# Loading and storing the sample caches of layer B from SyncE's queue, in 112 and 15 rows

## The chip, the core and the metric

The kernel runs on one core of a Trainium2 chip. The metric is the device time of one execution in microseconds (us). The engines are TensorE (PE in the profile, with PEld for its weight loads), VectorE (DVE), ScalarE (ACT), GpSimd (POOL) and SyncE (SP, which here issues DMAs and nothing else). "q" behind an engine's name means its queue of instructions, with the waits and the DMA issues.

## The reference

One inference step of a two-layer decoder trunk with width 1024, for a prompt of 1024 tokens and for 8 sample sequences with one new token each; both groups share the weights. All 1032 tokens go through the same matrix products.

```
layer A: x += hgrn2_mixer(rmsnorm(x)) @ w_a_out;  x += sq_relu_mlp(rmsnorm(x))
k, v = split(rmsnorm(x) @ w_kv)                      # 4 heads of 64
layer B: q = rmsnorm(x) @ w_b_q                      # 16 heads of 64
  prompt: attention over a sliding window of 128, T5 bias, a sink per head
  sample: kk = concat(cache_k_win, k_new); vv = concat(cache_v_win, v_new)
          the same attention over the last 128 rows
          cache_k_win_sample, cache_v_win_sample = kk[:, 1:], vv[:, 1:]
  x += attention @ w_b_out;  x += sq_relu_mlp(rmsnorm(x))
y = rmsnorm(x)
```

The sample caches have the shape (8, 128, 4, 64) in float32. The new window of a sequence is rows 1 to 127 of its old cache and one new row. It is read by the sample's attention and is also an output.

## The kernel before, in words

Tiles are 128 rows by 1032 tokens, with the model width on the partitions. A matrix product in float32 is made of three products of split operands (`job`, L386: high by high, low by high, high by low). The weights go from DRAM into two raw buffers (`load_raw`, L165, issued by SP), are split by ACT and DVE (L181 and L182 with a norm's gain, L186 and L189 without) into a pool of five units, and are read by PE.

The stage around the change is layer B's attention, about 1300 to 1640 us of the span. Its dense work is a list of steps: the products for K, V and the eight query groups, then `first_pass` (the first half of the w_b_out product). `mix` lays a list of side steps between them. The side steps come from `ticks(m, extra)`, one tick for each query group m of two heads, with eight blocks of 128 queries each: `scores(B)` (PE at L1193, then DVE and ACT), `turn(B - 3)` (PE transposes the probabilities, L1226; ACT and DVE split them, L1229 and L1230) and `weighted(B - 4)` (PE at L1244). For every two blocks `scores` ends with a reciprocal on DVE (L1212) and two multiplications of the probabilities by it on POOL (L1216). POOL also adds halves of the attention's output (L1254), loads the bias tiles (L1180), and writes the prompt's caches (L1128) and the new rows of the samples to a DRAM tile `newrows` (L1129).

`extras` (L1369) puts the sample's work into the ticks. In tick 4, `window` (L1265) is called four times, for K and V and for each half of the batch (four sequences). It takes a tile `win` with the 128 window rows on the partitions and four sequences of 256 columns side by side, loads 127 rows from the cache (L1270) and the last row from `newrows` (L1271). In tick 5 come `keys_t` (transposes of the windows of K, L1289), the scores and the products with the windows of V (`av`, L1319) for the first half of the heads, and `window_out` for K, which stores the whole tile to the output (L1274). In tick 6 come the stores of V, in tick 7 the second half of the heads. All these DMAs are issued by POOL.

In layer A and in the MLPs the order on PE, DVE and ACT is that of the source. In this stage it is not: `order.close()` (L1095) hands it to the framework's planner until L1388. The planner places the instructions of each queue by modelled times when the kernel is built, and each queue then runs in that order and waits where an operand is not there.

Of the kernel before, what the change touches and what calls it, by code (L numbers as in the profile page):

```python
# [9 lines left out]
F32 = mybir.dt.float32  # L10
# [7 lines left out]
P = 128  # L18
# [24 lines left out]
def trunk(ctx: ExitStack, tc: tile.TileContext, x_prompt, x_sample, state_hgrn, cache_k, cache_v,  # L43
# [4 lines left out]
    V, S, G, PE, SY = nc.vector, nc.scalar, nc.gpsimd, nc.tensor, nc.sync  # L48
# [8 lines left out]
    def uid(name):  # L57
        n_tile[0] += 1
        return f"{name}_{n_tile[0]}"

    def A(dt=F32, name="a"):
        return ap.tile([P, T], dt, tag="a", name=uid(name))
# [1043 lines left out]
    newrows = dp.tile([2, NS, 2 * P], F32, name="newrows")  # L1106
# [152 lines left out]
    win, smp = {}, {}  # L1259
    caches = {"k": (cache_k, 0, kc_sample), "v": (cache_v, 1, vc_sample)}  # L1260

    def tb(t):
        return t[:, :1024].rearrange("p (b c) -> p b c", c=256)

    def window(which, i):  # L1265
        cache, n, _ = caches[which]
        t = A(F32, "win")
        win[which, i] = t
        bs = slice(4 * i, 4 * i + 4)
        G.dma_start(out=tb(t)[0:P - 1], in_=cache[bs, 1:P].rearrange("b t h d -> t b (h d)"))  # L1270
        G.dma_start(out=tb(t)[P - 1:P], in_=newrows[n:n + 1, bs, :])  # L1271

    def window_out(which, i):
        G.dma_start(out=caches[which][2][4 * i:4 * i + 4].rearrange("b t h d -> t b (h d)"), in_=tb(win[which, i]))  # L1274

    def sample_steps(jt):

# [88 lines left out]
    def split_head(m):  # L1366
        heads_a[m] = split(aTs[m])

    extras = {4: [lambda w=w, i=i: window(w, i) for w in "kv" for i in range(2)],  # L1369
              5: s0[:2] + s1[:2] + s0[2:] + [lambda i=i: window_out("k", i) for i in range(2)],  # L1370
              6: [lambda i=i: window_out("v", i) for i in range(2)] + [lambda m=m: split_head(m) for m in range(NK // 2)],
              7: s1[2:5]}
    side = ticks(NK - 1, extras[NK - 1])
# [147 lines left out]
```

## Time and profile before

| | |
|---|---|
| Median of 3 runs | 2416.85 us (2414.13 to 2417.04) |
| Profiled execution, its own time | 2414.3 us |
| Its span, first to last instruction | 2412.6 us |
| PE busy | 2322.5 us, 96% of the span |
| DVE busy | 1619.8 us, 67% |
| ACT busy | 935.2 us, 39% |
| POOL busy | 231.2 us, 10% |

The busy time of an engine is the time in which one of its instructions runs. Issuing a DMA is not counted as busy on the page, but it appears in the timelines with the time that it held its engine. The granted clock is the share of TensorE's full clock of 2.4 GHz that the throttle allowed. A share of the whole span says little on a stage of 100 us; for that, the views are cut into windows.

### The profile page before, as it was taken

Reading aid. Unit: us, or ns where it says so; the run is one execution under the profiler, and the core shown is the slowest. Engines: PE = TensorE matmul, PEld = TensorE weight load, DVE = VectorE, ACT = ScalarE, POOL = GpSimd, SP = SyncE. Lnnn points to the kernel's source line nnn. Section 1 sums busy time; section 2 is a strip of 40 time slices with the busy share of each in tenths; the row PEclk is TensorE's granted clock in tenths of the full one; section 3 lists DMA queues with packets and bytes.
Section 4 is the critical chain, followed back from the end, with each engine's and each line's share of the span. In section 5 each row is a group of like instructions: output and inputs, shape, how many; then the busy total and the mean of one; then the engine's idle time right before and its main releaser. Section 6 shows DMA issues by size and latency. Waiting matters only on the chain. (4 is left out here: it accounts for less than half of the span.)

```text
span 2412.6 us, 40091 instructions
## 1 busy us (share of the span) xinstructions
PE 2322.5 (96%) x16389; PEld 2288.8 (95%) x16389; DVE 1619.8 (67%) x3154; ACT 935.2 (39%) x1914; POOL 231.2 (10%) x221
## 2 busy tenths in 40 slices
PE   8999999999999999999999995799999999999998
PEld 7899999999999999999999985699999999999998
DVE  5666676675476676766757884686467677676765
ACT  6444454543323322322325684564323223322322
POOL 0111111120000000000000245340000000000002
PEclk9999999999999999999999998899999999999999
DMA  3222222234111121111121112201111111121122
GB/s 124 72 63 63 63 63 64 72 70 73 44 45 53 44 57 49 45 53 45 53 62 45 42 37 48 65 27 40 40 45 53 53 54 44 45 62 45 44 62 80
DMA packets 206392, 133.23 MB, mean 55 GB/s; under 512 B 18122, under 2 KB 198532, under 8 KB 206208
## 3 DMA queue, kind: packets, MB, share of 16 engines
q1 hardware_dynamic: 186464, 107.04, 15.1%
q0 software_dynamic: 19392, 23.04, 4.2%
q8 instruction: 129, 2.11, 0.4%
q10 hardware_dynamic: 352, 0.59, 0.1%
q14 instruction: 55, 0.45, 0.1%
HBM read 115.97 MB, written 14.50 MB: 54 GB/s over the span
## 5 line engine op out<-in xcount | busy, mean ns | idle before, releaser
L386 PE MATMUL ps<-h,w 128*128 128x344 f32 (+1 forms) x6144 | 1161.8, 323 | 8.4 <-DVE y L882 3.1
L386 PEld LDWEIGHTS ps<-h,w 128*128 128x128 f32 x6144 | 996.3, 189 | 15.2 <-issue 8.7
L386 PE MATMUL ps<-l,w 128*128 128x344 f32 x3072 | 659.3, 322 | 2.6 <-DVE tmp L424 2.6
L386 PEld LDWEIGHTS ps<-l,w 128*128 128x128 f32 x3072 | 511.9, 189 | 4.3 <-DVE tmp L424 3.2
L1013 DVE TENSOR_TENSOR y<-ps,y 128x516 f32<-128x516 f32 x392 | 271.2, 692 | 125.6 <-PE ps L1008 123.1
L1008 PE MATMUL ps<-l,w 128*128 128x258 f32 x1120 | 226.0, 283 | 0.0
L1008 PE MATMUL ps<-b,w 128*128 128x258 f32 x1568 | 225.1, 283 | 0.0
L1022 DVE SCALAR_TENSOR_TENSOR r<-ps,R 128x688 f32<-128x688 f32 x126 | 81.7, 690 | 209.1 <-PE ps L386 209.1
L1008 PE MATMUL ps<-t,w 128*128 128x258 f32 x1344 | 218.5, 285 | 0.0
L219 ACT ACTIVATE w<-wr 128x512 fp32r<-128x512 f32 x168 | 99.6, 623 | 292.3 <-DVE wr L231 218.5
L1028 ACT ACTIVATE r<-r 128x1032 f32<-128x1032 f32 x63 | 67.3, 1068 | 367.6 <-DVE r L1022 367.6
L1008 PEld LDWEIGHTS ps<-b,w 128*128 128x128 f32 x1568 | 205.5, 190 | 0.0
L1008 PEld LDWEIGHTS ps<-t,w 128*128 128x128 f32 x1344 | 185.0, 190 | 0.3
L1008 PEld LDWEIGHTS ps<-l,w 128*128 128x128 f32 x1120 | 173.9, 190 | 0.0
L186 ACT ACTIVATE w<-wr 128x512 fp32r<-128x512 f32 x168 | 102.5, 622 | 132.3 <-PE ps L1008 74.6
L189 DVE TENSOR_TENSOR w<-wr,w 128x512 fp32r<-128x512 f32 x168 | 115.9, 708 | 54.5 <-ACT w L186 54.4
L182 DVE SCALAR_TENSOR_TENSOR w<-wr,cols,w 128x128 fp32r<-128x128 f32 x352 | 127.0, 403 | 30.7 <-ACT w L181 30.1
L227 DVE TENSOR_TENSOR w<-wr,w 128x512 fp32r<-128x512 f32 x168 | 115.3, 686 | 42.4 <-ACT w L219 42.3
L231 DVE TENSOR_TENSOR wr<-wr 128x256 f32<-128x256 f32 x280 | 118.0, 422 | 6.2
L181 ACT ACTIVATE w<-wr,cols 128x128 fp32r<-128x128 f32 x352 | 115.3, 393 | 12.7 <-PE ps L386 10.2
L963 ACT ACTIVATE t<-r 128x1032 fp32r<-128x1032 f32 x56 | 59.6, 1065 | 91.4 <-DVE r L985 91.4
L1461 POOL TENSOR_TENSOR sqc<-sqc,sq 128x384 f32<-128x384 f32 (+1 forms) x18 | 16.7, 927 | 749.1 <-ACT sq L1460 745.8
(295 smaller groups left out, 2731.7 us busy)
## 6 DMA issues: line engine op xcount, KB each, us to landing
wr<-in_w_up_dram SPq DMA_DIRECT2D x64, 512.0 KB, 4.2
wr<-in_w_down_dram SPq DMA_DIRECT2D x112, 256.0 KB, 3.1
wr<-in_w_a_in_dram SPq DMA_DIRECT2D x32, 512.0 KB, 4.2
si<-in_state_hgrn_dram POOLq DMA_DIRECT2D x8, 512.0 KB, 4.7
xin<-in_x_prompt_dram SPq DMA_DIRECT2D x8, 512.0 KB, 6.1
vb<-vrows POOLq DMA_DIRECT2D x8, 512.0 KB, 4.0
out_dram<-si POOLq DMA_DIRECT2D x8, 512.0 KB, 4.2
wr<-in_w_a_out_dram SPq DMA_DIRECT2D x8, 512.0 KB, 3.6
```

The source lines that it names most:

```text
L181: S.activation(out=hi[:, j], in_=part[:, j], func=AF.Copy, scale=g[:, k:k + 1])
L182: V.scalar_tensor_tensor(out=lo[:, j], in0=part[:, j], scalar=g[:, k:k + 1], in1=f32(hi[:, j]), op0=ALU.mult, op1=ALU.subtract)
L186: S.activation(out=hi, in_=part, func=AF.Copy)
L189: V.tensor_tensor(out=lo, in0=part, in1=f32(hi), op=ALU.subtract)
L219: S.activation(out=hi, in_=src, func=AF.Copy)
L227: V.tensor_tensor(out=lo, in0=src, in1=f32(hi), op=ALU.subtract)
L231: return lambda: V.tensor_tensor(out=out, in0=in0, in1=in1, op=op)
L386: PE.matmul(st["o"][c], lhsT=ww[:, col:col + P], rhs=xx[:, cs], start=((k, i) == first and also is None), stop=((k, i) == last))
L1008: PE.matmul(o[:, c, :CQ], lhsT=ww, rhs=xx[:, c * CQ:(c + 1) * CQ], start=(begins and k == 0 and i == 0), stop=(k == 1 and i == 2), skip_gr ...
L1013: V.tensor_tensor(out=y, in0=o[:, :, :CQ], in1=y, op=ALU.add)
L1022: V.scalar_tensor_tensor(out=v(r), in0=p, scalar=0.0, in1=v(R), op0=ALU.max, op1=ALU.mult)
L1028: S.activation(out=rs[-1], in_=rs[-1], func=AF.Square)
```

## The change

Three edits. `window` issues its load from SP instead of POOL, and as two DMAs, of 112 rows and of 15 rows, instead of one of 127. The copy of the new row moves from `window` into a function of its own, `window_new`, also on SP; in tick 4 the four calls of `window` come first and then the four of `window_new`, where before each copy followed its load. `window_out` issues its store from SP. The bytes and the tiles are the same.

```diff
--- before.py
+++ after.py
@@ -1263,15 +1263,18 @@
         return t[:, :1024].rearrange("p (b c) -> p b c", c=256)
 
     def window(which, i):
-        cache, n, _ = caches[which]
-        t = A(F32, "win")
+        cache, t = caches[which][0], A(F32, "win")
         win[which, i] = t
         bs = slice(4 * i, 4 * i + 4)
-        G.dma_start(out=tb(t)[0:P - 1], in_=cache[bs, 1:P].rearrange("b t h d -> t b (h d)"))
-        G.dma_start(out=tb(t)[P - 1:P], in_=newrows[n:n + 1, bs, :])
+        for r in (slice(0, 112), slice(112, P - 1)):
+            SY.dma_start(out=tb(t)[r], in_=cache[bs, r.start + 1:r.stop + 1].rearrange("b t h d -> t b (h d)"))
+
+    def window_new(which, i):
+        n = caches[which][1]
+        SY.dma_start(out=tb(win[which, i])[P - 1:P], in_=newrows[n:n + 1, 4 * i:4 * i + 4, :])
 
     def window_out(which, i):
-        G.dma_start(out=caches[which][2][4 * i:4 * i + 4].rearrange("b t h d -> t b (h d)"), in_=tb(win[which, i]))
+        SY.dma_start(out=caches[which][2][4 * i:4 * i + 4].rearrange("b t h d -> t b (h d)"), in_=tb(win[which, i]))
 
     def sample_steps(jt):
 
@@ -1366,7 +1369,7 @@
     def split_head(m):
         heads_a[m] = split(aTs[m])
 
-    extras = {4: [lambda w=w, i=i: window(w, i) for w in "kv" for i in range(2)],
+    extras = {4: [lambda w=w, i=i, f=f: f(w, i) for f in (window, window_new) for w in "kv" for i in range(2)],
               5: s0[:2] + s1[:2] + s0[2:] + [lambda i=i: window_out("k", i) for i in range(2)],
               6: [lambda i=i: window_out("v", i) for i in range(2)] + [lambda m=m: split_head(m) for m in range(NK // 2)],
               7: s1[2:5]}
```

## Rows read from the trace of the kernel before

**Rows 1.** The page's slices: PE's busy tenths and its granted clock, 60.3 us a slice.

```profile
PE   8999999999999999999999995799999999999998
...
PEclk9999999999999999999999998899999999999999
```

**Rows 2.** Stretches of 1470 to 1541 us; columns are in the first row.

```profile
core 0: us, PE busy (x) PEld busy (x) DVE busy (x) ACT busy (x) POOL busy (x), PEclk, DMA share, GB/s
...
1470.10:1494.60 24.50, 0.00 (x1) 0.00 (x0) 1.75 (x9) 2.17 (x9) 6.54 (x5) 0.60 0.20 41
1494.60:1507.20 12.60, 12.56 (x78) 12.28 (x78) 5.79 (x22) 8.32 (x25) 10.03 (x8) 0.83 0.35 70
1507.20:1522.60 15.40, 0.03 (x1) 0.00 (x0) 2.84 (x9) 0.70 (x2) 2.62 (x4) 0.57 0.25 70
1522.60:1541.40 18.80, 18.75 (x128) 18.09 (x129) 13.97 (x44) 12.83 (x38) 9.19 (x11) 0.90 0.32 111
```

**Rows 3.** Waits from 1440 to 1560 us: total, times, longest.

```profile
PE ps L1226 <- POOL pr L1216: 40.0, 2, 24.5
...
POOL win L1270 <- issue: 17.9, 1, 17.9
...
POOL out_dram L1274 <- issue: 15.1, 1, 15.1
```

**Rows 4.** POOL's timeline: start, duration, instruction, idle time before it.

```profile
1460.41 4.62 POOL L1270 DMA_DIRECT2D win<-in_cache_k_win_dram  x1
...
1466.31 4.62 POOL L1270 DMA_DIRECT2D win<-in_cache_k_win_dram  x1
...
1489.33 4.58 POOL L1270 DMA_DIRECT2D win<-in_cache_v_win_dram  x1 [17.89 <-issue]
1493.98 1.60 POOL L1216 TENSOR_TENSOR pr<-pr,es 128x256 f32<-128x256 f32 x2
...
1496.94 2.04 POOL L1216 TENSOR_TENSOR pr<-pr,es 128x512 f32<-128x512 f32 x2
1498.92 4.64 POOL L1270 DMA_DIRECT2D win<-in_cache_v_win_dram  x1
...
1519.92 1.58 POOL L1274 DMA_DIRECT2D out_dram<-win  x2 [15.08 <-issue]
1521.56 2.03 POOL L1216 TENSOR_TENSOR pr<-pr,es 128x512 f32<-128x512 f32 x2
```

**Rows 5.** DVE's timeline: the reciprocals of the softmax denominators.

```profile
1468.51 0.16 DVE L1212 RECIPROCAL es<-es 128x4 f32<-128x4 f32 x1
...
1472.50 0.18 DVE L1212 RECIPROCAL es<-es 128x4 f32<-128x4 f32 x1
...
1504.92 0.16 DVE L1212 RECIPROCAL es<-es 128x4 f32<-128x4 f32 x1
```

**Rows 6.** DMA issues: count, size of each, median us from issue to landing.

```profile
wr<-in_w_b_out_dram SPq DMA_DIRECT2D x8, 512.0 KB, 3.4
...
win<-in_cache_k_win_dram POOLq DMA_DIRECT2D x2, 508.0 KB, 29.0
win<-in_cache_v_win_dram POOLq DMA_DIRECT2D x2, 508.0 KB, 29.9
...
newrows<-rows POOLq DMA_DIRECT2D x4, 4.0 KB, 2.1
win<-newrows POOLq DMA_DIRECT2D x4, 4.0 KB, 23.9
```

**Rows 7.** SP's longest wait, its weight load at 1500 us, and ACT's first read of it.

```profile
SPq L165 <- DVE w L182: 66.4, 2, 49.4
...
1500.64 0.37 SPq L165 DMA_DIRECT2D wr<-in_w_b_out_dram  x1
...
1555.29 0.62 ACT L186 ACTIVATE w<-wr 128x512 fp32r<-128x512 f32 x1
```

**Rows 8.** Readers of the windows on PE: duration min/median/max ns, first and last start.

```profile
L1319 PE MATMUL ps<-win,qz x32: 272/273/323, 1544.3 to 1603.4; 128*64 128x128 f32 x32
...
L1289 PE MATMUL ps<-ident,win x16: 272/272/273, 1530.9 to 1534.1; 128*128 128x128 f32 x16
```

## The prediction

> **What bounds the kernel now.** I read the page's slices first. The reader is to see TensorE (PE) at nine tenths or more nearly everywhere, one dip around slices 24 to 26, and a granted clock of 0.8 to 0.9 beside it [rows 1]. The dip lies at 1450 to 1570 us, inside layer B's attention stage. Everything else is a full PE, which this change does not touch, so the question is what the dip is worth and what would take its place.
>
> The table of stretches cuts the dip at PE's own stops [rows 2]. From 1470.1 to 1494.6 us PE does nothing, from 1507.2 to 1522.6 us again nothing; between and behind these it is full. DVE and ACT are idle there as well, 1.75 and 2.17 us busy in the first stop, 2.84 and 0.70 us in the second. No arithmetic engine is the limit.
>
> The waits say who is [rows 3]. PE's transposes of the probabilities (L1226) waited 40.0 us in two pieces for POOL's multiplication by 1/denominator (L1216). POOL itself shows 17.9 us ahead of a window load (L1270) and 15.1 us ahead of a window store (L1274), both put down to "issue": nothing in the profile that it waited for.
>
> POOL's timeline puts them in order [rows 4]. Two K loads are issued at 1460.41 and 1466.31 us, 4.62 us each. The first V load starts at 1489.33, the multiplication behind it at 1493.98, and PE resumes at 1494.64. The reciprocals that those multiplications need were done by DVE at 1468.51 and 1472.50 us, and that of the second stop at 1504.92 [rows 5]; their multiplications ran at 1493.98, 1496.94 and 1521.56. So the data were 17 to 25 us early and POOL late.
>
> Why POOL stood still can be read from the DMA table [rows 6]: a window load takes 29.0 (K) or 29.9 us (V) from issue to landing. 1460.41 + 29.0 = 1489.4, where POOL's first stop ends (1489.33); 1489.33 + 29.9 = 1519.2, where its second ends (1519.92). It looks as if POOL's queue holds about two such loads, and the next waits until the oldest lands. The 4 KB of new rows take 23.9 us, so they too land only when a window load in front of them does.
>
> **What the change removes.** From POOL go four loads (4 x 4.6 us of issue), four copies of new rows and four stores, and with them both waits. I count at PE, since that sets the end: 24.5 + 15.4 = 39.9 us [rows 2]. It comes off whole if POOL then reaches each multiplication before PE runs dry. It does: with reciprocals at 1468.51 and 1504.92 and some 0.6 and 1.0 us for the first of two multiplications (from 1493.98 to PE's restart at 1494.64, from 1521.56 to 1522.64), PE's operands stand at about 1469.3 and 1506.0, ahead of 1470.1 and 1507.2.
>
> Second term, the clock. Behind each stop PE runs for a while at the lower level: a mean granted clock of 0.83 over 12.6 us and 0.90 over 18.8 us [rows 2]. With 0.5 of full (1.2 of 2.4 GHz) as the lower level that is 2 x 0.17 x 12.6 = 4.3 us and 2 x 0.10 x 18.8 = 3.8 us at half rate, so half of 8.1, **4.0 us**, was lost and comes back when the stops go.
>
> Third term, what PE meets instead. While PE stood, DVE still worked 1.75 + 2.84 = 4.6 us of backlog, which PE may now have to wait for. Bounds: 0 (it is work for later steps) and 4.6 us. No row is nearer to either end; I take the middle, **2.3**.
>
> **What it adds on SP.** SP gets eight partial loads, four copies of new rows and four stores: 16 x 0.37 us of issue [rows 7] = 5.9 us. I cost it at nothing, because SP idles in front of its weight buffers: one of its waits in 1440 to 1560 us is 49.4 us long. Queued behind these DMAs are the loads of w_b_out. The one issued at 1500.64 us lands 3.4 us later and is first read by ACT at 1555.29 (the splits before that are those of the load in front of it) [rows 6, 7]: 51 us of cover, against 5.9 us of issue and some 2 MB of transfers. Were that cover gone, PE would wait for weights by the excess.
>
> The landing of a 112-row load from SP is shown by no row. Bounds: 3.4 us, a weight load of 512 KB from SP, and 29.9 us, the present window load [rows 6]. I take 3.4, the row with the same queue and about the same bytes; the 15 rows at most as much again, the new rows 2.1 us (newrows<-rows). The whole set is then through in 4 x (3.4 + 3.4) + 4 x 2.1 = 36 us if nothing overlapped, and much less if SP keeps several in flight.
>
> When is it wanted? The key transposes (L1289) run at 1530.9 us, the products with the values (L1319) from 1544.3 [rows 8]. With 39.9 + 4.0 = 43.9 us gone these come at 1487 and 1500. Loads issued from 1460 on, as now, have 27 us before the keys; that is enough with any overlap. New in the order is that K's new rows come behind all four V loads, so the keys now wait for V's transfers too.
>
> The Trainium skill, "DMA: Bandwidth & Descriptors", section "Issuing engines are not separate DMA queues", speaks against the change: DMAs of all issuers run on the same 16 DMA engines, and another issuer saves only issue time, usually little. The section "Why a DMA increments its semaphore by 16 and not by 1" of the same page of the Trainium skill speaks for the split: the number of engines is the largest up to 16 that divides the slowest dimension, so 127 rows get one, 112 rows 16 and 15 rows 15, and the new loads would land like weight loads. The 29 us for 508 KB beside 3.4 us for 512 KB agrees with that for 127; no row here shows 112.
>
> **The sum.** All terms are taken from one execution. 2414.3 (the profiled execution; its span is 2412.6) - 39.9 - 4.0 + 2.3 = **2372.7 us**. The median of the runs shown is 2416.85, 2.5 above that execution, so I put the forecast between, at **2374 us**.
>
> **The rivals.**
>
> *The keys wait for SP.* SP's wait of 49.4 us stands in front of the weight load of 1500.64, which without the first stop comes at about 1476. In this stage the planner, not the source, orders each queue. Put behind that load, the window loads go out from 1476, and the new rows of K land after four loads of up to 6.8 us (3.4 + 3.4) and two copies of 2.1: 1507 us, 20 us after the keys are wanted. That gives 2372.7 + 20 = 2393. For it: SP's queue runs in order and its waits are long. Against: the window loads come earlier in the source than that weight load is needed.
>
> *Slower: SP's loads run as narrowly as POOL's and one after the other.* If each 112-row load takes 112/127 of 29.0 us = 25.6 us in one lane, four take 102 us; the new rows land at 1460 + 102 = 1562, 75 us after the keys are wanted, and the time is 2372.7 + 75 = 2448. It decides from the point where the 41.6 us of the sum are used up: four loads of more than 69 us (1487 + 42 - 1460), 17 us each. Against: every 512 KB weight load from SP lands in a fifth of that.
>
> *Only issue time comes off.* If the waits follow the window loads to their readers, what goes from PE's stops is the issue time inside them: 4.6 us (1489.33 to 1493.98), 0.8 us of the second K load (1470.1 to 1470.93) and 1.6 us of two stores [rows 4]. 2414.3 - 7.0 = 2407.3. The section of the Trainium skill on issuing engines, named above, would have it so. Against this rival: reciprocals, not windows, feed the multiplication that PE waits for, and the keys are wanted 27 us after the first load.
>
> *Nothing changes*, if POOL's stops have another cause than the DMAs in front of them: 2414. Two ends of waits that fall within 0.7 us of a landing speak against it.
>
> **How the numbers follow.** The forecast's case has 0.74, with its own range of 2366 to 2382: all backlog hidden and a slightly better plan below, all 4.6 us of it paid and a slightly worse plan above. The keys' wait has 0.13, issue time alone 0.04, a new plan of the whole stage that loses some 20 us elsewhere 0.03, no change 0.02, slower 0.04. The range is 2364 to 2394: it holds the first two cases and leaves out the rest, with a margin for the plan. A measurement of this kernel can tell about 0.2%, 4.8 us, from no change: faster 0.94, same 0.02, slower 0.04.
>
> **What would show it.** POOL's timeline without a wait above 10 us between 1455 and 1550 us, with each multiplication (L1216) within 2 us of its reciprocal; PE without a stop above 5 us there and with a granted clock of 1.0; landings of the window loads of 3 to 7 us from SP; the whole stage behind it as now, 42 us earlier. The forecast is wrong if PE stops at the key transposes or at the products with the values (rival one or two), if weight splits wait for their loads, or if the new plan puts another wait in front of the transposes of the probabilities.

## The result, and the profile after

The changed kernel takes 2375.9 us in the median of four runs (2374.8 to 2378.3), against 2415.8 us before; the ratio is 0.984, with a 95% interval of 0.982 to 0.985. The profiled execution took 2378.25 us, with a span of 2376.5 us.

The page's slices of the changed kernel, PE's busy tenths and its granted clock, answer to [rows 1]:

```profile
PE   8999999999999999999999999999999999999998
...
PEclk9999999999999999999999999999999999999999
```

The dip is gone. How large it was is best read from the stage as a whole, from the last copy of new rows to DRAM (L1129) to the last residual of the first half of w_b_out (L861). The first fence is the kernel before, the second the changed one with four of its slices of 10 us; columns are in the first row.

```profile
core 0: us, PE busy (x) PEld busy (x) DVE busy (x) ACT busy (x) POOL busy (x), PEclk, DMA share, GB/s
1455.90:1647.60 191.70, 146.23 (x999) 139.02 (x998) 128.18 (x375) 103.50 (x284) 79.47 (x69) 0.89 0.17 45
```

```profile
1458.00:1612.90 154.90, 146.77 (x1000) 140.32 (x1000) 131.38 (x376) 103.44 (x284) 55.52 (x57) 0.97 0.19 55
1460.00:1470.00 10.00, 8.62 (x54) 8.13 (x53) 9.12 (x23) 6.67 (x17) 2.99 (x3) 0.88 0.85 209
1470.00:1480.00 10.00, 9.69 (x69) 9.40 (x69) 8.03 (x29) 9.49 (x34) 5.18 (x6) 0.95 0.53 180
...
1520.00:1530.00 10.00, 7.87 (x48) 7.39 (x48) 9.23 (x21) 7.57 (x18) 2.12 (x2) 0.83 0.00 0
...
1550.00:1560.00 10.00, 8.55 (x51) 7.94 (x52) 8.63 (x23) 3.02 (x12) 1.23 (x1) 0.83 0.00 0
```

The stage went from 191.7 to 154.9 us, 36.8 less. PE's busy time in it is the same within 0.6 us; its idle time fell from 191.70 - 146.23 = 45.5 to 154.90 - 146.77 = 8.1 us, by 37.3. The span fell by 36.1: the changed kernel's execution reached the stage 2.1 us later (1458.0 against 1455.9), and was already 2.0 us late at 523.3 us (POOL's DMAs of L157, 521.3 before), in code that is the same in both; it needed 1.4 us less behind it.

POOL's timeline shows the multiplications (L1216) that stood in [rows 4], and DVE's the reciprocals of [rows 5]:

```profile
1472.05 1.61 POOL L1216 TENSOR_TENSOR pr<-pr,es 128x256 f32<-128x256 f32 x2 [6.52 <-DVE es L1212]
...
1476.88 2.10 POOL L1216 TENSOR_TENSOR pr<-pr,es 128x512 f32<-128x512 f32 x2 [2.40 <-DVE es L1212]
...
1481.88 2.04 POOL L1216 TENSOR_TENSOR pr<-pr,es 128x512 f32<-128x512 f32 x2 [2.09 <-DVE es L1212]
...
1487.97 2.03 POOL L1216 TENSOR_TENSOR pr<-pr,es 128x512 f32<-128x512 f32 x2 [0.81 <-ACT w L186]
```

```profile
1471.72 0.16 DVE L1212 RECIPROCAL es<-es 128x4 f32<-128x4 f32 x1
...
1476.55 0.16 DVE L1212 RECIPROCAL es<-es 128x4 f32<-128x4 f32 x1
...
1481.54 0.17 DVE L1212 RECIPROCAL es<-es 128x4 f32<-128x4 f32 x1
...
1487.61 0.17 DVE L1212 RECIPROCAL es<-es 128x4 f32<-128x4 f32 x1
```

Each multiplication now starts 0.33 to 0.36 us behind its reciprocal; before, it was 17 to 25 us. No idle time on POOL is put down to "issue" any more.

SP's timeline: all eight partial loads go out within 4.3 us, and the stores can start at 1468.14, so the first window with its new row had landed within 12 us of the first issue. The DMA table has landings for two of the kinds.

```profile
1456.28 2.09 SPq L1270 DMA_DIRECT2D win<-in_cache_k_win_dram  x4
1458.41 2.18 SPq L1270 DMA_DIRECT2D win<-in_cache_v_win_dram  x4
1460.70 3.26 SPq L1274 DMA_DIRECT2D win<-newrows  x4
1468.14 3.30 SPq L1277 DMA_DIRECT2D out_dram<-win  x4
```

```profile
out_dram<-win SPq DMA_DIRECT2D x4, 512.0 KB, 5.0
...
win<-in_cache_v_win_dram SPq DMA_DIRECT2D x2, 60.0 KB, 8.2
```

PE's remaining waits in the stage, and the readers of the windows, which answer to [rows 3] and [rows 8]:

```profile
PE ps L1193 <- DVE qs L1176: 7.0, 8, 1.5
PE ps L1244 <- ACT ph L1229: 0.4, 2, 0.2
```

```profile
L1322 PE MATMUL ps<-win,qz x32: 272/273/323, 1507.0 to 1568.7; 128*64 128x128 f32 x32
...
L1292 PE MATMUL ps<-ident,win x16: 272/272/273, 1494.4 to 1497.4; 128*128 128x128 f32 x16
```

The longest wait of PE is 1.5 us, for the split queries (L1176). The keys are transposed at 1494.4 us, 26 us after SP began its stores.

### The profile page after: what moved, and what is told of

It reads as the page before. It is cut to its first block, busy times and chain, and to the rows that moved or that the text cites. A ratio compares the mean times of both kernels' runs of the same rounds, so it can differ in the third digit from the quotient of the medians.

```text
span 2376.5 us, 40102 instructions
## 1 busy us (share of the span) xinstructions
PE 2324.6 (98%) x16389; PEld 2290.8 (96%) x16389; DVE 1622.9 (68%) x3154; ACT 935.6 (39%) x1914; POOL 207.1 (9%) x209
## 5 line engine op out<-in xcount | busy, mean ns | idle before, releaser
L181 ACT ACTIVATE w<-wr,cols 128x128 fp32r<-128x128 f32 x352 | 115.2, 392 | 11.9 <-PE ps L386 10.2
```

What stands on the lines that cost most here:

```text
L181: S.activation(out=hi[:, j], in_=part[:, j], func=AF.Copy, scale=g[:, k:k + 1])
```

## The experiments

Theory A: 127 rows run in one lane, that is, on one of the core's 16 DMA engines, so a window load takes 29 us; POOL's queue takes about two of those, and the next DMA holds POOL with all that is behind it. It says that the split is what helps. Theory B: POOL's queue is the limit, and the move to SP is what helps. The two parts of the change were tried one at a time, then the queue's depth, then the terms of the sum that came out wrong. Ratios are to the kernel before on the same chip, with 95% intervals.

### The move without the split

```diff
-        for r in (slice(0, 112), slice(112, P - 1)):
+        for r in (slice(0, P - 1),):
             SY.dma_start(out=tb(t)[r], in_=cache[bs, r.start + 1:r.stop + 1].rearrange("b t h d -> t b (h d)"))
```

> The changed kernel with each window loaded by SP as one DMA of 127 rows instead of 112 and 15. Theory A (POOL's stops came from window loads that take 29 us because 127 rows run in one lane, and the split is what makes them fast): on SP the four loads run one after the other in one lane, 4 x 29 = 116 us from 1456 us, the new rows land behind them at about 1574, the key transposes wanted at 1494 wait some 80 us, and SP's stores wait in front of the weight loads: 2376 + 80 = 2456 us, about 2440 to 2500, slower than the kernel before. Theory B (the queue is what matters, any load from SP is as fast as a weight load): 2376 us, as with the split.

It took 2430.7 us, ratio 1.005 (1.004 to 1.007): slower than the kernel before. SP's timeline and one wait of PE:

```profile
1454.05 19.77 SPq L1270 DMA_DIRECT2D win<-in_cache_k_win_dram  x2
1473.87 44.09 SPq L1270 DMA_DIRECT2D win<-in_cache_v_win_dram  x2
1518.06 22.98 SPq L1274 DMA_DIRECT2D win<-newrows  x4
1546.12 3.29 SPq L1277 DMA_DIRECT2D out_dram<-win  x4
```

```profile
PE ps L1292 <- DMA win<-newrows: 54.7, 1, 54.7
```

The loads issue one after the other, and SP itself is held by them: two DMAs of K last 19.8 us in its queue, those of V 44.1, the copies of new rows 23.0. The stores start at 1546.12, so the four windows took 92 us from 1454.05, 23 us each, and the key transposes waited 54.7 us for a new row. Theory A, with 23 us for each load in place of the 29 that it expected; the loss was smaller by that, and the time came out below the 2440 to 2500 us that were expected. Theory B falls. This is the second rival of the prediction, which the split kept away.

The lanes can be counted in the profile: the last column but one of a stretch is the mean busy share of the 16 DMA engines. The first fence is the kernel before with two window loads under way, the second this run.

```profile
1480.00:1490.00 10.00, 0.00 (x0) 0.00 (x0) 0.00 (x0) 0.00 (x0) 0.67 (x1) 0.50 0.14 46
```

```profile
1510.00:1520.00 10.00, 0.00 (x0) 0.00 (x0) 0.00 (x0) 0.00 (x0) 0.00 (x0) 0.50 0.07 24
```

0.14 x 16 = 2.2 engines for POOL's two loads, 0.07 x 16 = 1.1 for SP's, at some 23 GB/s for each: one lane for a load, two loads at a time on POOL and one on SP. In the changed kernel the share is 0.96 to 0.99 from 1458 to 1462 us.

### The split without the move

```diff
-        G.dma_start(out=tb(t)[0:P - 1], in_=cache[bs, 1:P].rearrange("b t h d -> t b (h d)"))
+        for r in (slice(0, 112), slice(112, P - 1)):
+            G.dma_start(out=tb(t)[r], in_=cache[bs, r.start + 1:r.stop + 1].rearrange("b t h d -> t b (h d)"))
```

> The kernel before with only the split: POOL issues each window as 112 and 15 rows, everything else as before. Theory A (slow landing is the cause of POOL's stops): the loads land in under 10 us, POOL's waits of 17.9 and 15.1 us go, its issue time (4 x 4.6 us or somewhat more) stays in front of the multiplications and costs PE up to 5 us at one or two places: 2378 to 2392 us. Theory B (POOL's own queue is the limit, however the rows are cut): the waits stay, 2405 to 2420 us.

It took 2381.0 us, ratio 0.985 (0.983 to 0.987). The DMA table and, from the tile's instructions, the time for which one issue holds POOL (min, median and max in ns):

```profile
win<-in_cache_k_win_dram POOLq DMA_DIRECT2D x2, 448.0 KB, 4.3
win<-in_cache_v_win_dram POOLq DMA_DIRECT2D x2, 448.0 KB, 5.1
```

```profile
L1271 POOL DMA_DIRECT2D win<-in_cache_k_win_dram x4: 572/668/775, 1462.3 to 1467.1; - x4
```

The same queue, cut at 112 rows, lands 448 KB in 4.3 to 5.1 us instead of 508 KB in 29 [rows 6], and POOL has no wait above 0.2 us put down to issue. Theory A. What it did not foresee is that the issue itself falls too, from 4.62 us [rows 4] to 0.67.

### Only K on POOL, with 127 rows

```diff
-        for r in (slice(0, 112), slice(112, P - 1)):
-            SY.dma_start(out=tb(t)[r], in_=cache[bs, r.start + 1:r.stop + 1].rearrange("b t h d -> t b (h d)"))
+        for r in (slice(0, P - 1),) if which == "k" else (slice(0, 112), slice(112, P - 1)):
+            (G if which == "k" else SY).dma_start(out=tb(t)[r], in_=cache[bs, r.start + 1:r.stop + 1].rearrange("b t h d -> t b (h d)"))
...
-        SY.dma_start(out=tb(win[which, i])[P - 1:P], in_=newrows[n:n + 1, 4 * i:4 * i + 4, :])
+        (G if which == "k" else SY).dma_start(out=tb(win[which, i])[P - 1:P], in_=newrows[n:n + 1, 4 * i:4 * i + 4, :])
```

> The changed kernel, but the two K windows load from POOL as before (127 rows, then the new row); V's loads and all stores are on SP. Theory A with its reading that POOL's queue takes about two such loads before it waits: only the third DMA waited, so POOL issues both K loads (4.6 us each) without a wait; its next DMA, a bias load at about 1487 us, comes as the first K load lands: at most a few us of wait, 2376 to 2384 us. Rival (every slow window load stops POOL, the number does not matter): one stop of some 20 us of PE remains, 2396 to 2402 us.

It took 2381.5 us, ratio 0.985 (0.984 to 0.987). POOL's timeline:

```profile
1461.76 4.62 POOL L1270 DMA_DIRECT2D win<-in_cache_k_win_dram  x1
...
1467.13 4.59 POOL L1270 DMA_DIRECT2D win<-in_cache_k_win_dram  x1
...
1490.81 0.78 POOL L1180 DMA_DIRECT2D bias<-scr  x1 [5.92 <-issue]
```

Two slow loads alone do not stop POOL. The next DMA, a bias load, waited 5.9 us and started at 1490.81, where the first K load lands by its median (1461.76 + 28.8 = 1490.6). The two copies of new rows in between (4 KB each) were issued without a wait; the next DMA behind them is held, and it holds only what comes behind it on POOL. PE waited 2.8 us for that multiplication and 3.2 us for K's new rows.

The number of slow DMAs alone does not set the limit. Earlier in the kernel before, POOL issued seven DMAs of another shape (384 KB each, 25 to 46 us to landing) one after the other without a wait:

```profile
521.30 7.46 POOL L157 DMA_DIRECT2D scr<-vrow  x7
```

The eighth followed after 24.5 us. What POOL's queue counts stays open; two is shown for window loads of 127 rows.

### Only the stores on SP

```diff
-        G.dma_start(out=caches[which][2][4 * i:4 * i + 4].rearrange("b t h d -> t b (h d)"), in_=tb(win[which, i]))
+        SY.dma_start(out=caches[which][2][4 * i:4 * i + 4].rearrange("b t h d -> t b (h d)"), in_=tb(win[which, i]))
```

> The kernel before with only the stores moved to SP; the loads stay on POOL with 127 rows. The first stop (17.9 us on POOL, 24.5 us at PE) must stay whole. Theory A: the second stop belonged to the store as POOL's next DMA behind two outstanding window loads; without it POOL goes on until its next DMA, a bias load some 5 to 8 us later, which then waits for the first V load: of the second 15.4 us between 5 and 15 go, 2400 to 2411 us. Rival (the second stop belongs to the V loads themselves): nothing goes, 2414 to 2418 us.

It took 2406.3 us, ratio 0.995 (0.994 to 0.997), as theory A has it. POOL's timeline and PE's waits for it:

```profile
1489.11 4.58 POOL L1270 DMA_DIRECT2D win<-in_cache_v_win_dram  x1 [17.96 <-issue]
...
1518.97 0.79 POOL L1180 DMA_DIRECT2D bias<-scr  x1 [10.79 <-DVE mx L1202]
1519.83 2.03 POOL L1216 TENSOR_TENSOR pr<-pr,es 128x512 f32<-128x512 f32 x2
```

```profile
PE ps L1226 <- POOL pr L1216: 29.2, 2, 24.6
```

The first stop is whole (18.0 us on POOL, 24.6 at PE). The second has moved to the bias load, which started at 1518.97, 29.9 us behind the first V load; PE lost only 29.2 - 24.6 = 4.6 us there: the multiplication that had stood behind the store [rows 4] ran at 1505.32, 0.3 us behind its reciprocal, and only the next one stood. The profile puts POOL's wait down to a reduction on DVE (L1202), but the last one of that query group had ended at 1508.9, ten us before; in the changed kernel the same DMA starts 0.3 us behind it. That the wait ends at the landing is inferred from the 29.9 us.

### The new rows directly behind their loads

```diff
-    extras = {4: [lambda w=w, i=i, f=f: f(w, i) for f in (window, window_new) for w in "kv" for i in range(2)],
+    extras = {4: [lambda w=w, i=i, f=f: f(w, i) for w in "kv" for i in range(2) for f in (window, window_new)],
```

> The changed kernel with each copy of a new row directly behind its window load, as in the kernel before, instead of all four at the end. All windows with their new rows have landed by about 1468 us in the changed kernel, 26 us before the key transposes, so the order should not matter: within 0.2% of the changed kernel, 2372 to 2380 us. Rival (V's copies wait on SP for the new rows of V and hold up the loads behind them): SP waits some 3 us, still hidden; only if the plan changes would the time leave that range.

It took 2376.4 us, ratio 0.984 (0.982 to 0.985), beside 2377.1 us for the changed kernel on the same chip. The order of the copies is worth nothing that can be measured: the windows are early either way.

### The changed kernel again, twice

No edit.

> The changed kernel once more, as the base for the runs beside it and for a second profile. Time 2375 to 2378 us. If the places where PE's granted clock falls in the attention stage belong to the planned waits for the split queries (L1193 waiting for L1176), they appear again at the same instructions; if they are chance, they lie elsewhere or are gone.

> The changed kernel a third time, beside the two below: 2374 to 2378 us. In the two profiles so far the attention stage (last copy of new rows on POOL to the last residual of first_pass) took 154.9 and 153.5 us, of which PE lost 4.7 and 1.6 us to half clock. If the clock's falls are chance and not the plan's, this profile has another sum again, and the stage less that loss is 150 to 152 us as in both.

They took 2377.1 us, ratio 0.984 (0.983 to 0.985), and 2375.3 us, ratio 0.983 (0.982 to 0.985). The stage in the first and in the second, each with its only slice of 10 us below full clock:

```profile
1459.30:1612.80 153.50, 144.73 (x1000) 137.19 (x1000) 130.95 (x375) 103.42 (x284) 55.54 (x57) 0.99 0.18 55
...
1550.00:1560.00 10.00, 8.63 (x52) 7.95 (x53) 8.77 (x23) 3.00 (x12) 1.23 (x1) 0.83 0.00 0
```

```profile
1456.90:1610.30 153.40, 144.63 (x1002) 137.29 (x1000) 131.27 (x376) 103.39 (x284) 55.53 (x57) 0.99 0.19 56
...
1490.00:1500.00 10.00, 9.19 (x62) 8.74 (x62) 8.14 (x23) 4.91 (x16) 1.64 (x3) 0.83 0.00 1
```

PE's loss to half clock is estimated as its busy time times what is missing of the clock. In the first profile of the changed kernel, four slices give 8.62 x 0.12 + 9.69 x 0.05 + 7.87 x 0.17 + 8.55 x 0.17 = 4.3 us; here 8.63 x 0.17 = 1.5 and 9.19 x 0.17 = 1.6. The stage without it is 150.6, 152.0 and 151.8 us.

In the timelines of PE each fall (to 0.50 of full, the lower level) begins at or just behind a pair of waits for the split queries (L1193 for L1176), two pauses of 0.5 to 1.5 us close together. There are four such pairs, at the same instructions in all three executions; in the first they end at 1466.7, 1493.7, 1524.7 and 1552.6 us. The clock fell behind the first, third and fourth pair in the first profile, behind the fourth alone in the second, and at the second alone in the third. So the places are those of the plan, but whether the clock falls at one differs from execution to execution, and with it some 3 us of the time; why is not shown.

### The queries split in two halves

```diff
-                S.activation(out=t[own, :SEQ], in_=q[own, :SEQ], func=AF.Copy)
-                V.tensor_tensor(out=t[other, :SEQ], in0=q[own, :SEQ], in1=f32(t[own, :SEQ]), op=ALU.subtract)
-                qs.append(t)
+                qs.append((t, own, other))
+            for c in HALF:
+                for t, own, other in qs:
+                    S.activation(out=t[own, c], in_=q[own, c], func=AF.Copy)
+                    V.tensor_tensor(out=t[other, c], in0=q[own, c], in1=f32(t[own, c]), op=ALU.subtract)
```

> The changed kernel with the split of each query group (ACT L1175, DVE L1176) done in two halves of 512 columns instead of one piece of 1024, so that the first block of scores can start after the first half. Theory: PE's eight waits for DVE there (7.0 us in the changed kernel) shorten by about half, and with them the stretches at half clock behind them (about 5 us lost): 2368 to 2373 us. Rival (16 more instructions on a DVE that is 85 to 90% busy in this stage cost as much, or the waits only move): 2374 to 2380 us.

It took 2381.9 us, ratio 0.985 (0.984 to 0.987), no better than the changed kernel (2377.1 on the same chip) and above the range of the rival too. PE's waits in the stage; the edit shifts the lines, and L1198 stands for L1193, L1179 for L1176, L1249 for L1244:

```profile
PE ps L1198 <- DVE qs L1179: 3.9, 6, 0.9
PE ps L1249 <- DVE pl L1235: 2.4, 4, 1.6
PE ps L1304 <- DVE qz L1182: 1.2, 1, 1.2
```

The waits for the queries did halve, from 7.0 to 3.9 us, but others took their place: 2.4 us for the split probabilities and 1.2 us for the samples' queries, neither of them above 0.3 us before. All of PE's waits in the stage come to 11.3 us against 8.1, and DVE is busy for 134.3 us of the stage instead of 131.4. The clock did not fall in this stage, and the time was still no better. The queries before tick 4 are split as well: from the first copy of new rows to the last, ahead of the stage, the kernel took 137.5 us against 132.9. So the rival is nearer, and more waits came than went; that DVE is too full for them to go is argued, not shown.

### Five lanes instead of sixteen, and the split on POOL once more

```diff
-        for r in (slice(0, 112), slice(112, P - 1)):
+        for r in (slice(0, 125), slice(125, P - 1)):
```

> The changed kernel with the windows cut as 125 and 2 rows. By the Trainium skill, DMA: Bandwidth & Descriptors, section Why a DMA increments its semaphore by 16 and not by 1, 125 rows run on 5 engines and 112 on 16. If the number of rows decides how many lanes a load gets, the 125-row load lands clearly later than the 112-row one, though sooner than the 29 us of 127 rows: at the 17.5 GB/s of one lane (508 KB in 29 us), 500 KB on five lanes take about 6 us alone and some 23 us for all four. That is still about in time for the keys: 2375 to 2385 us. If the number of rows does not matter, the landings are those of the changed kernel.

> The changed kernel with 125 and 2 rows, now timed. Its loads are slower (all stores can start at 1475 instead of 1468 us) but still 16 us ahead of the key transposes, so it should not differ from the changed kernel; the 2373.5 us of its one run is then the absence of any fall of the clock in that execution: 2373 to 2378 us. Rival (slower loads spread the traffic and help): 2 us or more below the changed kernel.

A single execution took 2373.5 us, just under the range expected, and the median of four more 2374.5 us, ratio 0.983 (0.982 to 0.984). SP's timeline, and then the stage and four microseconds of the loads, from the profile of the second run:

```profile
1454.55 5.59 SPq L1270 DMA_DIRECT2D win<-in_cache_k_win_dram  x4
1460.18 9.56 SPq L1270 DMA_DIRECT2D win<-in_cache_v_win_dram  x4
1469.85 1.15 SPq L1274 DMA_DIRECT2D win<-newrows  x4
1475.53 3.29 SPq L1277 DMA_DIRECT2D out_dram<-win  x4
```

```profile
1456.30:1608.10 151.80, 143.05 (x1000) 135.64 (x999) 130.80 (x375) 103.37 (x284) 55.51 (x57) 1.00 0.18 56
...
1464.30:1468.30 4.00, 3.37 (x27) 3.31 (x28) 3.72 (x14) 2.94 (x10) 0.00 (x0) 1.00 0.34 121
```

The loads issue over 15.2 us instead of 4.3, and the stores start 21.0 us behind the first issue instead of 11.9: slower than 112 rows, far faster than 127, which is what the rule on the number of engines in the Trainium skill, "DMA: Bandwidth & Descriptors", section "Why a DMA increments its semaphore by 16 and not by 1", would make of 125 rows. The DMA share agrees: 0.34 x 16 = 5.4 engines. The time of the whole cannot be told from that of the changed kernel. Neither of the two profiles has a slice below full clock; whether the slower loads have to do with that, or four other profiles were unlucky, stays open.

> The kernel before with the split alone, all on POOL, once more beside the changed kernel. If the queue is worth something by itself, as POOL's issue time (8 x 0.67 us of loads, 4 x 0.53 and 4 x 0.77 us) still delays multiplications that PE waits for, this stays 2 to 5 us above the changed kernel; if not, the two cannot be told apart (within 0.1%).

The split on POOL took 2379.4 us this time, ratio 0.985 (0.984 to 0.986), beside 2375.3 us. Its stage:

```profile
1459.10:1615.60 156.50, 146.49 (x1002) 139.08 (x1000) 131.88 (x375) 103.49 (x284) 66.53 (x73) 0.98 0.18 55
```

PE is idle for 156.5 - 146.5 = 10.0 us here and for 8.1 to 8.8 us in the profiles of the changed kernel. Twice now the split on POOL has come out above the changed kernel, by 2.7 us as the ratios have it the first time (0.9848 against 0.9837) and by 4.1 us here; the intervals of the ratios overlap, so the move to SP is worth some 0.1 to 0.2%, if anything.

## Why the prediction was right

The forecast was 2374 us, the median is 2375.9; 39.8 us came off the medians and 36.1 off the profiled executions, where the sum had 41.6. By its steps:

**The cause.** Right. POOL's stops were the next DMA behind two slow window loads, held until the older one landed. Both ends were tested: with only two slow loads on POOL, no stop of more than 6 us; with the loads left and only the stores gone, the first stop whole and the second at the next DMA. The "two" holds for these loads only: of another kind of DMA (L157) POOL took seven.

**The stops, 39.9 us.** Right, and they came off whole: no wait of PE for L1216 above 0.2 us is left, and idle time in the stage fell by 37.3 us.

**What PE meets instead, 2.3 us.** Right in size, by luck: the 39.9 us came to 37.3 of idle time, 2.6 less, but 2.3 was the middle of two bounds, and it is not the backlog that was named: the waits for the split queries (L1176) grew from 4.1 to 7.0 us.

**The clock, 4.0 us.** This term was mis-sized. It took for granted that the clock stays full once the long stops are gone, and the prediction's signs asked for 1.0. In the changed kernel it fell again, behind pairs of pauses of at most 1.5 us each, and PE lost 4.3 us there in the profiled execution and 1.5 and 1.6 in two more. Before, the same reckoning gives 12.56 x 0.17 + 18.75 x 0.10 = 4.0 us [rows 2]. So between nothing and 2.5 us of the term came back in those three executions; in the profiled one PE's busy time in the stage even rose by 0.5 us. Its time (2378.25) lies 5.5 us above the sum (2372.7): 4.5 for this term (PE's busy time +0.5 instead of -4.0), 0.3 for the one before, and 2.1 - 1.4 = 0.7 from outside the stage.

**SP's 16 issues at nothing.** Right. They took SP 2.09 + 2.18 + 3.26 + 3.30 = 10.8 us with the waits between them, more than the 5.9 reckoned, and PE waits for no weight. The first rival, that the windows stand behind the weight load that waits, did not come: they were issued from 1456.28, before it.

**The landing.** The bound taken (3.4 us for each part) was too low for the 60 KB parts, 8.2 us in the median behind and among the other loads (for 112 rows from SP the table has no landing), but the first window was complete 12 us behind the first issue and the last store went out at 1470.3, 14 us behind it, where 36 had been allowed.

**The rivals.** The slower one is real and belongs to the move without the split: 92 us for four loads, where the prediction had put the turning point at 69, and a loss of 13.3 us (2430.7 against 2417.5). That only issue time comes off (2407 us) is refuted by the split alone: 2381.0 us with every DMA still issued by POOL. The rule of the Trainium skill that spoke against the change, in "DMA: Bandwidth & Descriptors", section "Issuing engines are not separate DMA queues", is borne out for the move beside the split (0.1 to 0.2%, not clear of noise). It says nothing of the split, which brought nearly all, nor of the loss that the move brought without it. The prediction weighed the two together and would not have said which part mattered.

## What to carry to other kernels

Look at the landing time of each DMA beside its bytes: 508 KB in 29 us next to 512 KB in 3.4 us is a load that runs narrow, and a row count such as 127 can be cut into 112 and 15 at the price of one more DMA issue (0.3 to 0.8 us here). The share of busy DMA engines in a stretch with nothing else under way says how narrow. A slow DMA costs little by itself; it costs when a later DMA on the same queue is held and an engine's arithmetic stands behind that one. Change the shape before the queue: moved to SP uncut, the same loads made this kernel slower than it had been.

## What the runs showed of the hardware, unexpectedly

- One issue of the 127-row load held POOL for 4.6 us, one of 112 rows for 0.67.
- SP is held as well: with one-lane loads outstanding, a single DMA issue sat in its queue for up to 22 us, against 0.3 to 0.8 us for the split loads.
- In one lane, SP's four loads took 23 us each, one after the other (DMA share 0.07); POOL's took 29 us, two at a time (0.14).
- POOL was held behind two window loads of 127 rows, but issued seven DMAs of 384 KB and 39 us to landing in a row.
- Behind the same four pairs of pauses of 0.5 to 1.5 us, PE's granted clock fell at three, one, one and none of them in four executions (the last with windows of 125 and 2 rows).
